# Which queue issues the loads: weights, sample cache and mixing operands from ScalarE instead of SyncE

## The chip, the cores and the metric

The kernel runs on one core of one Trainium2 chip. The metric is the device time of one execution in microseconds; the kernel before took 1886.35 us (median of 3 runs: 1886.35, 1886.42 and 1881.0).

A core has TensorE (PE in the profile; PEld are its weight loads), VectorE (DVE), ScalarE (ACT), GpSimd (POOL) and SyncE (SP). Each engine works off its own instructions in the order in which they stand in its program, and an instruction that waits holds back all that stand behind it on its engine. A transfer is also such an instruction: it is issued by an engine, in its place in that engine's program, and then runs on the 16 DMA engines. The profile writes SPq for transfers issued by SyncE.

## The reference, cut to what matters

One step of a hybrid decoder layer on 1024 prompt positions and 8 x 4 = 32 sample positions (T = 1056 columns in all), model width 2048. One input projection yields q, k, v, an attention gate, and u, vc and a gate for a chunked gMLP. Sixteen heads of 64 attend with three dilated causal windows, merged by their denominators; the sample rows also see a cache of 2048 past keys and values. The gated outputs go through an output projection, a residual and an RMSNorm.

```python
z = _rms_norm(x, norm_g) @ w_in
q, k, v, ga, u, vc, gb = jnp.split(z, SPLITS, axis=-1)
...
for window, d in DILATIONS:                     # (128, 1), (512, 4), (2048, 16)
    s = jnp.einsum('brnqhk,brnshk->brnhqs', qb, kcat) * scale
    p, lse = _softmax_lse(s, mask)
    o = jnp.einsum('brnhqs,brnshk->brnqhk', p, vcat)
return _combine(outs, lses)
...
mixed = jnp.einsum('gts,bcsgk->bctgk', _masked_spatial(w_s), vr) + jnp.transpose(b_s)[:, :, None]
return u * mixed.reshape(B, S, D_CHUNK)
...
a = o_attn.reshape(B, T, D_ATTN).astype(x.dtype) * jax.nn.silu(ga)
c = o_chunk * jax.nn.silu(gb)
return x + jnp.concatenate([a, c], axis=-1) @ w_out
```

## The kernel before, in words

**Projections.** Every product is made of fp16 parts: a float32 operand is split into a high part (ScalarE) and a low part (VectorE), and three matmuls replace one. The input projection has 56 tiles of 128 output columns, the output projection 16. A tile is three chunks of 352 positions (`proj_chunk`, L181), each of 48 matmuls: 144 a tile. Its weights come as two raw halves of 512 KB (`w_load`, tile `wraw`, three buffers, L120) and are split in four parts (`w_split`: `wh` on ScalarE L138, `wl` on VectorE L139). `run_m` loads the first half for the tile after next at a tile's start; the second half of tile m + 1 is loaded inside `w_split` of tile m, after its part 1.

**Steps between the matmuls.** All other work is cut into steps with a cost each (`set_steps`); after every 6 projection matmuls `fill` runs as many steps as their costs allow. This gives the program's order. The framework's scheduler then orders each engine's instructions by that priority and by when it believes their operands ready, and it puts an instruction with low priority ahead where an engine would else be idle.

**Periods.** Tiles of the input projection are grouped by head pair. From the first pair's end on, a period (six tiles at first, five in two of the last) projects gates, u and v of one pair (`run_m`), then the q/k halves of a pair, tiles x and y, side by side (`run_ab`, with the rotation `rope`, L470 to L477, after every chunk). Beside these matmuls run:
- the prompt's attention of the pair before, 16 items (8 query tiles x 2 heads), one a slot: `fa` makes scores (L611, L612, tile `s`), the row minimum (L620) and the exponential (ACT L632); `fb` normalizes, splits (`pn`, L146 and L147) and transposes the probabilities by DMA (`pt`, L648, four buffers); `fc` multiplies them with the values into the one PSUM bank `o` (L659, L666) and evacuates it (ACT `ot` L670, DVE `onat` L671). `fc` runs three slots after `fa`; `gate` (L677) follows when both heads are there.
- the sample's attention in x and y (`sample_steps`): `load` brings 8 key and 8 value blocks of 448 KB (`kvr`, two buffers, L712); `prep` splits one (keys `kvh` on ScalarE L720, values on GpSimd L722, then `kvl` on VectorE L723; three buffers each) and at its end loads the block after next; `s_mm` makes the scores (L751, L752), `soft1` and `soft2` the softmax (L774 to L799, ending in the DMA transposes `pst`), `pv_new` (L808) and `pv_mm` (L819, L820) the value products, `fin` the result.
- the mixing of the gMLP: `mix_load` brings eight pieces `vr` (L858) and three small operands (L867 to L869).
- at the end of `run_ab`, `stack_load` (L500 to L504) reads back the rotated q and k of the pair from DRAM into `qst`, `khd` and `klo`, with which the next prompt attention begins.

**Queues.** All transfers are issued by SyncE, in one order: loads, stores and DMA transposes.

Of the kernel before, what the change touches and what calls it, by code (L numbers as in the profile page):

```python
# [54 lines left out]
def hybrid_step_kernel(  # L55
# [25 lines left out]
    nc = tc.nc  # L81
    PE, ACT, DVE, POOL, SP = nc.tensor, nc.scalar, nc.vector, nc.gpsimd, nc.sync

    def pool(name, stack=ctx, bufs=1, **kw):
# [27 lines left out]
    def w_load(m, half=0, parts=1):  # L112
# [5 lines left out]
        for i in range(parts):  # L118
            c = slice(i * n, (i + 1) * n)
            SP.dma_start(  # L120
                out=t.rearrange("p a b -> p (a b)")[:, c], in_=src[:, half * KT * 64 + i * n:half * KT * 64 + (i + 1) * n]
            )
        w_raw[m, half] = t

    def w_split(m, part):
# [15 lines left out]
        )  # L141
        if part == 1:
            w_load(m + 1, 1)
# [442 lines left out]
    ap_ = pool("ap", right, side="right")  # L586
    msk = ap_.tile([64, NKEY + NS], F32, name="msk")
    trl = ap_.tile([128, 160], F32, name="trl")
    SP.dma_start(out=msk, in_=mask_s)
    SP.dma_start(out=trl, in_=tril)  # L590
# [4 lines left out]
    def prompt_steps(p):  # L595
# [90 lines left out]
        n = len(items)  # L686
        for s in range(n + 4):
            fs = []
            cost = 1.2 if s > 4 else 2.0
            if s - 4 >= 0 and (s - 4) % 2 == 1:  # L690
                fs.append(lambda t=(s - 4) // 2: gate(t))
            if 0 <= s - 3 < n:
                fs.append(lambda i=s - 3: fc(i))
                cost += 0.04 * (items[s - 3][0] + 1)
            if 0 <= s - 1 < n:
                fs.append(lambda i=s - 1: fb(i))
            if s < n:
                fs.append(lambda i=s: fa(i))
                cost += 0.04 * (items[s][0] + 1)
            slots.append((cost, lambda fs=fs: [f() for f in fs]))  # L700
        return slots, ahl

    def sample_steps(p, ahl):
        raws = {}
        sts = {}

        def load(j):
            if j >= 2 * DB:
                return
            t = ap_.tile([128, NKEY], F32, tag="kvr", name="kvr", bufs=2)  # L710
            src = kc if j < DB else vc
            SP.dma_start(out=t, in_=src[p, :, j % DB])  # L712
            raws[j] = t

        def prep(j):
# [10 lines left out]
            sts[j] = (hi, lo)  # L726
            load(j + 2)

        cur = {}

# [30 lines left out]
        def soft1():  # L761
            stsb = cur["st"]
            ss = ap_.tile([128, S], F32, tag="sp", name="ss", bufs=2)[0:64, 0:NKEY + NS]
            prev = 3e38
            for g in range(2):
# [17 lines left out]
                )  # L783
                prev = mn[0:64]
            den = ap_.tile([128, 1], F32, tag="den", name="den", bufs=6)
            ACT.activation(out=ss, in_=ss, func=AF.Exp, scale=-1.0, bias=prev, accum_out=den[0:64])
# [35 lines left out]
        def fin():  # L822
            o = cur["o"]
            a = ap_.tile([128, 64], F32, tag="oa", name="oa", bufs=1)
            b = ap_.tile([128, 64], F32, tag="ob", name="ob", bufs=1)
            ACT.activation(out=a, in_=o[:, 64:128], func=AF.Copy)
# [15 lines left out]

        pre = [(0.05, lambda: load(0)), (0.05, lambda: load(1))]
        s1 = [(0.1, lambda: prep(0)), (0.1, lambda: prep(1)), (0.2, s_new), wait(0.8)]
# [10 lines left out]
    def vr_load(g, half):  # L855
        vr = ap_.tile([128, 4, 2, 128], F16, tag="vr", name="vr", bufs=2)
        for i in range(4):
            SP.dma_start(out=vr[:, i], in_=vr_d[half * 4 + i, :, :, g * 128:(g + 1) * 128])  # L858
        return vr

    def mix_load(g):
# [4 lines left out]
        gs = slice(g * 128, (g + 1) * 128)  # L866
        SP.dma_start(out=vrs, in_=vr_d[NQ, 0:NS, :, gs])  # L867
        SP.dma_start(out=wr, in_=wst[g])
        SP.dma_start(out=bb, in_=bst[g].partition_broadcast(128))  # L869
        mixs[g] = (vr, vrs, wr, bb)  # L870
# [428 lines left out]
```

## Time and profile before

| | |
|---|---|
| median of 3 runs | 1886.35 us (1881.0 to 1886.42) |
| the profiled execution's own time | 1881.56 us |
| its span, first to last instruction | 1879.8 us |
| mean granted TensorE clock | 0.995 |
| TensorE busy | 1790.0 us (95%) |
| VectorE busy | 1085.5 us (58%) |
| ScalarE busy | 724.5 us (39%) |
| GpSimd busy | 125.2 us (7%) |
| transfers | 276.13 MB, 56.3% of 16 DMA engines' span on SyncE's queue |

Busy times don't count the issuing of transfers. Times within the execution are given in us from the span's start. In the view of waits a row names the engine and line that waited, what ended the wait, and the total in us, the number of times and the longest one. In the timeline a row has its start, its duration, engine, line, operation, output and inputs, a count, and in brackets the idle time of the engine before it and what ended it. A wait for several things is put down to the one that came last.

### The profile page before, as it was taken

To read this page: it belongs to the slowest core of one execution; us is meant where nothing else is said; L and a number is where in the kernel's file an instruction comes from. 1 tells how busy PE (TensorE), PEld (TensorE's weight loads), DVE (VectorE), ACT (ScalarE), POOL (GpSimd) and SP (SyncE) were. 2 spreads that over 40 slices of the span, in tenths; PEclk is the share of its full clock that TensorE was granted. 3 is DMA by queue.
4 is the path that set the end of the run, shared out by engine and by line. 5 is a ranking of instruction groups with operands and counts; after the bars stand their busy time and mean duration, and the time that the engine had idled before them with its cause. 6 is when DMAs were issued, how large, how long until landed. Compare 5 with 4: busy or idle time off the path is not lost. (4 is left out here: it accounts for less than half of the span.)

```text
span 1879.8 us, 37188 instructions
## 1 busy us (share of the span) xinstructions
PE 1790.0 (95%) x15040; PEld 1220.3 (65%) x15040; DVE 1085.5 (58%) x2392; ACT 724.5 (39%) x1605; POOL 125.2 (7%) x139
## 2 busy tenths in 40 slices
PE   8999998999999999999999999999989999999997
PEld 7866665666666666666666656666656666666667
DVE  7733696746665665665755566566566533324344
ACT  7522323632542453354244245245245311212134
POOL 0000010001001000100100100100100110000001
PEclk9999999999999999999999999999999999999999
DMA  7433346666656655656665666576675697222324
GB/s 260 118 81 68 81 135 184 122 166 172 147 117 180 180 120 162 191 115 154 172 157 125 160 202 116 149 210 130 165 197 110 178 336 190 68 68 68 77 59 185
DMA packets 340414, 276.13 MB, mean 147 GB/s; under 512 B 255889, under 2 KB 291729, under 8 KB 338129
## 3 DMA queue, kind: packets, MB, share of 16 engines
q1 hardware_dynamic: 340242, 273.76, 56.3%
q8 instruction: 117, 1.92, 0.4%
q14 instruction: 55, 0.45, 0.1%
HBM read 179.85 MB, written 38.26 MB: 116 GB/s over the span
## 5 line engine op out<-in xcount | busy, mean ns | idle before, releaser
L181 PE MATMUL proj<-xh,wh 128*128 128x352 f16 (+3 forms) x3712 | 1107.7, 303 | 6.2 <-DVE ta L475 2.9
L181 PE MATMUL proj<-xl,wh 128*128 128x352 f16 (+3 forms) x3712 | 1107.3, 303 | 1.5 <-DVE xl L147 1.5
L181 PE MATMUL proj<-xh,wl 128*128 128x352 f16 (+3 forms) x3712 | 1107.1, 303 | 0.4 <-DVE wl L139 0.4
L181 PEld LDWEIGHTS <-wh 128*128 128x128 f16 x7424 | 696.9, 98 | 325.4 <-issue 6.0
L181 PEld LDWEIGHTS <-wl 128*128 128x128 f16 x3712 | 362.6, 98 | 169.7 <-issue 1.9
L139 DVE SCALAR_TENSOR_TENSOR wl<-wraw,wh 128x512 f16<-128x512 f32 x288 | 202.3, 730 | 124.8 <-ACT wh L138 123.9
L138 ACT ACTIVATE wh<-wraw 128x512 f16<-128x512 f32 x288 | 165.8, 620 | 205.7 <-PE proj L181 198.7
L723 DVE SCALAR_TENSOR_TENSOR kvl<-kvr,kvh 128x896 f16<-128x896 f32 x128 | 143.0, 1117 | 95.3 <-ACT kvh L720 53.0
L632 ACT ACTIVATE sp<-sp,mn 128x256 f32<-128x256 f32 (+7 forms) x128 | 99.0, 773 | 150.6 <-DVE mn L620 150.6
L147 DVE SCALAR_TENSOR_TENSOR pn<-sp,pn 128x512 f16<-128x512 f32 (+2 forms) x192 | 106.4, 565 | 33.5 <-ACT pn L146 32.7
L722 POOL TENSOR_SCALAR kvh<-kvr 128x896 f16<-128x896 f32 x64 | 70.2, 1098 | 439.6 <-DMA kvr<-in_vc 272.2
L146 ACT ACTIVATE pn<-sp 128x512 f16<-128x512 f32 (+2 forms) x192 | 94.8, 516 | 11.4 <-DMA pt<-pn 8.4
L720 ACT ACTIVATE kvh<-kvr 128x896 f16<-128x896 f32 x64 | 60.7, 948 | 80.7 <-DMA kvr<-in_kc 46.4
L620 DVE CUSTOM_DVE_ANT_0 sp<-s,mp 128x512 f32<-128x512 f32 (+3 forms) x128 | 74.3, 584 | 21.6 <-PE s L612 20.1
L659 PE MATMUL o<-vst,pt 128*128 128x128 f16 x576 | 66.5, 220 | 21.0 <-DMA pt<-pn 17.4
L147 DVE SCALAR_TENSOR_TENSOR yhl<-proj,yhl 128x352 f16<-128x352 f32 (+1 forms) x42 | 21.4, 510 | 92.3 <-ACT yhl L146 92.3
L146 ACT ACTIVATE yhl<-proj 128x352 f16<-128x352 f32 (+1 forms) x42 | 18.8, 448 | 135.9 <-PE proj L181 116.5
L659 PEld LDWEIGHTS <-pt 128*128 128x128 f16 x576 | 52.1, 98 | 28.5 <-DMA pt<-pn 18.5
L639 DVE RECIPROCAL r<-den 128x1 f32<-128x1 f32 x128 | 20.8, 162 | 81.1 <-ACT sp L632 80.9
L666 PE MATMUL o<-vst,pt 128*128 128x64 f16 x576 | 63.0, 193 | 0.0
L923 POOL TENSOR_TENSOR gb<-gb,tb 128x352 f32<-128x352 f32 x24 | 28.8, 1201 | 511.4 <-DVE tb L203 511.4
L611 PE MATMUL s<-khd,qst 128*128 128x512 f16 (+2 forms) x192 | 61.7, 327 | 0.9 <-DVE mn L620 0.9
(165 smaller groups left out, 1562.6 us busy)
## 6 DMA issues: line engine op xcount, KB each, us to landing
wraw<-in_w_in SPq DMA_DIRECT2D x110, 512.0 KB, 4.5
kvr<-in_kc SPq DMA_DIRECT2D x64, 448.0 KB, 4.3
kvr<-in_vc SPq DMA_DIRECT2D x64, 448.0 KB, 4.0
wraw<-in_w_out SPq DMA_DIRECT2D x32, 512.0 KB, 5.1
yn<-in_x SPq DMA_DIRECT2D x8, 1024.0 KB, 9.2
out_y_p<-yn SPq DMA_DIRECT2D x16, 512.0 KB, 3.5
xn<-in_x SPq DMA_DIRECT2D x7, 1024.0 KB, 6.4
out_v_o<-tb SPq DMA_DIRECT2D x24, 176.0 KB, 2.5
```

What stands on the lines that cost most here:

```text
L138: ACT.activation(out=hi[:, sl, :], in_=r[:, rs, :], func=AF.Copy, scale=WS)
L139: DVE.scalar_tensor_tensor(out=lo[:, sl, :], in0=r[:, rs, :], scalar=WS, in1=hi[:, sl, :], op0=ALU.mult, op1=ALU.subtract)
L146: ACT.activation(out=hi, in_=src, func=AF.Copy, scale=scale)
L147: DVE.scalar_tensor_tensor(out=lo, in0=src, scalar=scale, in1=hi, op0=ALU.mult, op1=ALU.subtract)
L181: PE.matmul(out=ps[:, 0:n], lhsT=a[:, k, :], rhs=b[:, k, c0:c0 + n], start=(i == 0), stop=(i == 3 * KT - 1))
L611: PE.matmul(out=ps[:, 0:n], lhsT=qst[h][:, tq], rhs=khd[h][:, j0:j0 + n], start=True, stop=False)
L620: DVE.tensor_tensor_reduce(sp[:, j0:j0 + n], ps[:, 0:n], mp[:, S - nk + j0:S - nk + j0 + n], 1.0 / (QS * KS), prev, ALU.add, ALU.min, mn,)
L632: ACT.activation(out=sp[:, 0:nk], in_=sp[:, 0:nk], func=AF.Exp, scale=-1.0, bias=prev, accum_out=den)
L659: PE.matmul(out=o[:, 0:128].rearrange("p (l c) -> p l c", l=2), lhsT=pt[:, j], rhs=vst[:, :, kb, h * HD:(h + 1) * HD], start=(kb == 0), st ...
L666: PE.matmul(out=o[:, 0:64], lhsT=pt[:, w + j], rhs=vst[:, 0, kb, h * HD:(h + 1) * HD], start=False, stop=(kb == nb - 1))
L722: POOL.tensor_scalar(hi, r, VS, 1.0, ALU.mult, ALU.mult)
L723: DVE.scalar_tensor_tensor(out=lo, in0=r, scalar=KS if j < DB else VS, in1=hi, op0=ALU.mult, op1=ALU.subtract)
```

## The change

- The weight loads from the fifth tile on, the sample's key and value loads and the mixing loads are issued by ScalarE (`LQ`), at the places in its program where the scheduler puts them. Stores, DMA transposes and the loads of `stack_load` stay on SyncE.
- The second raw half of the weights is loaded after part 3 of the split instead of part 1.
- `kvr` gets a third buffer, so three key blocks are loaded ahead, and a `prep` of a key block loads the third block after it. The mask of the sample's softmax has no buffer of its own any more: it is loaded every period as the ninth block, into a `kvr` buffer. Three value blocks (the third to the fifth) are loaded by `soft1`, between its minima and its exponential, the last three by the preps of the third to the fifth.
- In the prompt attention, `fc` of the items 0 to 7 comes one slot later (four after `fa`), those of the items 8 to 15 stay at three, so that slot 11 has two (items 7 and 8). `gate` comes one slot later everywhere.
- In `fin` two small tiles share buffers with `ot` (left out below).

```diff
--- before.py
+++ after.py
@@ -80,6 +80,7 @@
 ):
     nc = tc.nc
     PE, ACT, DVE, POOL, SP = nc.tensor, nc.scalar, nc.vector, nc.gpsimd, nc.sync
+    LQ = ACT
 
     def pool(name, stack=ctx, bufs=1, **kw):
         return stack.enter_context(tc.tile_pool(name=name, bufs=bufs, **kw))
@@ -117,7 +118,7 @@
         n = KT * 64 // parts
         for i in range(parts):
             c = slice(i * n, (i + 1) * n)
-            SP.dma_start(
+            (SP if m < 4 else LQ).dma_start(
                 out=t.rearrange("p a b -> p (a b)")[:, c], in_=src[:, half * KT * 64 + i * n:half * KT * 64 + (i + 1) * n]
             )
         w_raw[m, half] = t
@@ -139,7 +140,7 @@
         DVE.scalar_tensor_tensor(
             out=lo[:, sl, :], in0=r[:, rs, :], scalar=WS, in1=hi[:, sl, :], op0=ALU.mult, op1=ALU.subtract
         )
-        if part == 1:
+        if part == 3:
             w_load(m + 1, 1)
 
     def hilo(src, hi, lo, scale):
@@ -584,9 +585,7 @@
 
     right = ExitStack()
     ap_ = pool("ap", right, side="right")
-    msk = ap_.tile([64, NKEY + NS], F32, name="msk")
     trl = ap_.tile([128, 160], F32, name="trl")
-    SP.dma_start(out=msk, in_=mask_s)
     SP.dma_start(out=trl, in_=tril)
 
     def wait(c):
@@ -684,14 +683,15 @@
 
         slots = []
         n = len(items)
-        for s in range(n + 4):
+        for s in range(n + 5):
             fs = []
             cost = 1.2 if s > 4 else 2.0
-            if s - 4 >= 0 and (s - 4) % 2 == 1:
-                fs.append(lambda t=(s - 4) // 2: gate(t))
-            if 0 <= s - 3 < n:
-                fs.append(lambda i=s - 3: fc(i))
-                cost += 0.04 * (items[s - 3][0] + 1)
+            if s - 5 >= 0 and (s - 5) % 2 == 1:
+                fs.append(lambda t=(s - 5) // 2: gate(t))
+            for i in range(n):
+                if s == i + (4 if i < 8 else 3):
+                    fs.append(lambda i=i: fc(i))
+                    cost += 0.04 * (items[i][0] + 1)
             if 0 <= s - 1 < n:
                 fs.append(lambda i=s - 1: fb(i))
             if s < n:
@@ -703,14 +703,19 @@
     def sample_steps(p, ahl):
         raws = {}
         sts = {}
+        cur = {}
 
         def load(j):
-            if j >= 2 * DB:
+            if j > 2 * DB:
                 return
-            t = ap_.tile([128, NKEY], F32, tag="kvr", name="kvr", bufs=2)
+            t = ap_.tile([128, NKEY + NS], F32, tag="kvr", name="kvr", bufs=3)
+            if j == DB:
+                LQ.dma_start(out=t[0:64], in_=mask_s)
+                cur["msk"] = t
+                return
             src = kc if j < DB else vc
-            SP.dma_start(out=t, in_=src[p, :, j % DB])
-            raws[j] = t
+            LQ.dma_start(out=t[:, 0:NKEY], in_=src[p, :, j if j < DB else j - DB - 1])
+            raws[j if j < DB else j - 1] = t[:, 0:NKEY]
 
         def prep(j):
             hi = ap_.tile([128, NKEY], F16, tag="kvh", name="kvh", bufs=3)
@@ -724,9 +729,10 @@
                 out=lo, in0=r, scalar=KS if j < DB else VS, in1=hi, op0=ALU.mult, op1=ALU.subtract
             )
             sts[j] = (hi, lo)
-            load(j + 2)
-
-        cur = {}
+            if j < DB:
+                load(j + 3)
+            elif j >= DB + 2:
+                load(j + 4)
 
         def s_new():
             stsb = cur["st"] = ap_.tile([128, NKT + 1, 64], F32, tag="stp", name="stsb", bufs=1)
@@ -760,6 +766,7 @@
 
         def soft1():
             stsb = cur["st"]
+            msk = cur["msk"][0:64]
             ss = ap_.tile([128, S], F32, tag="sp", name="ss", bufs=2)[0:64, 0:NKEY + NS]
             prev = 3e38
             for g in range(2):
@@ -782,6 +789,8 @@
                     mn[0:64],
                 )
                 prev = mn[0:64]
+            for i in (3, 4, 5):
+                load(DB + i)
             den = ap_.tile([128, 1], F32, tag="den", name="den", bufs=6)
             ACT.activation(out=ss, in_=ss, func=AF.Exp, scale=-1.0, bias=prev, accum_out=den[0:64])
             r = ap_.tile([128, 1], F32, tag="r", name="r", bufs=6)
...
@@ -840,7 +849,7 @@
             hilo(f[:, 0:NS], ahl[:, 0, S:T], ahl[:, 1, S:T], AS)
             SP.dma_start(out=act_d[p], in_=ahl)
 
-        pre = [(0.05, lambda: load(0)), (0.05, lambda: load(1))]
+        pre = [(0.05, lambda: load(0)), (0.05, lambda: load(1)), (0.05, lambda: load(2))]
         s1 = [(0.1, lambda: prep(0)), (0.1, lambda: prep(1)), (0.2, s_new), wait(0.8)]
         for b in range(DB):
             s1.append((0.4, lambda b=b: (s_mm(b), prep(b + 2))))
@@ -855,7 +864,7 @@
     def vr_load(g, half):
         vr = ap_.tile([128, 4, 2, 128], F16, tag="vr", name="vr", bufs=2)
         for i in range(4):
-            SP.dma_start(out=vr[:, i], in_=vr_d[half * 4 + i, :, :, g * 128:(g + 1) * 128])
+            LQ.dma_start(out=vr[:, i], in_=vr_d[half * 4 + i, :, :, g * 128:(g + 1) * 128])
         return vr
 
     def mix_load(g):
@@ -864,9 +873,9 @@
         wr = ap_.tile([128, 160], F32, tag="wr", name="wr", bufs=1)
         bb = ap_.tile([128, 160], F32, tag="bb", name="bb", bufs=1)
         gs = slice(g * 128, (g + 1) * 128)
-        SP.dma_start(out=vrs, in_=vr_d[NQ, 0:NS, :, gs])
-        SP.dma_start(out=wr, in_=wst[g])
-        SP.dma_start(out=bb, in_=bst[g].partition_broadcast(128))
+        LQ.dma_start(out=vrs, in_=vr_d[NQ, 0:NS, :, gs])
+        LQ.dma_start(out=wr, in_=wst[g])
+        LQ.dma_start(out=bb, in_=bst[g].partition_broadcast(128))
         mixs[g] = (vr, vrs, wr, bb)
 
     def mix_prep(g):
```

**ScalarE, the sample's softmax** (period of the fourth pair's x and y; `sa` are the two halves of the scores' sums, `ss` the exponential, `pn` its high part, `qkhl` the rotation's high part of a chunk). Before:

```order
L756 ACTIVATE sa<-s 128x224
L720 ACTIVATE kvh<-kvr 128x896 x3
L756 ACTIVATE sa<-s 128x224
L146 ACTIVATE qkhl<-o_9428 128x704
L786 ACTIVATE ss,den<-ss,mn 64x928
L146 ACTIVATE pn<-ss 64x928
L146 ACTIVATE qkhl<-o_9578 128x704
L138 ACTIVATE wh<-wraw 128x512 x4
```

Now:

```order
L762 ACTIVATE sa<-s 128x224
L147 ACTIVATE qkhl<-o_9428 128x704
L717 DMA kvr<-in_vc 128x896 x3
L795 ACTIVATE ss,den<-ss,mn 64x928
L717 DMA kvr<-in_vc 128x896
L147 ACTIVATE pn<-ss 64x928
L147 ACTIVATE qkhl<-o_9584 128x704
L717 DMA kvr<-in_vc 128x896 x2
L139 ACTIVATE wh<-wraw 128x512 x4
L121 DMA wraw<-in_w_in 128x1024 x2
```

Three value loads now stand ahead of the exponential and one between it and the high part of the probabilities. That one takes the buffer of the third value block, and waits for its `kvl`.

**VectorE, the same place.** Before:

```order
L774 ISA ss,mn<-t,msk,mn 64x416
L774 ISA mn 64x1
L788 RECIPROCAL r<-den 64x1
L789 TENSOR_SCALAR ss<-ss,r 64x928
L147 SCALAR_TENSOR_TENSOR pn<-ss,pn 64x928
```

Now:

```order
L781 ISA ss,mn<-t,kvr,mn 64x416
L781 ISA mn 64x1
L728 SCALAR_TENSOR_TENSOR kvl<-kvr,kvh 128x896
L471 TENSOR_TENSOR ta<-proj,cos_t 128x352
L797 RECIPROCAL r<-den 64x1
L798 TENSOR_SCALAR ss<-ss,r 64x928
L148 SCALAR_TENSOR_TENSOR pn<-ss,pn 64x928
```

The `kvl` of the third value block and one operation of the rotation have come between the minimum and the reciprocal.

**SyncE, the first prompt attention** (`pt` are the transposes of the probabilities). Before:

```order
L590 DMA trl<-in_tril 128x160
L858 DMA vr<-vr_d 128x2x128 x8
L867 DMA vrs<-vr_d 32x2x128
L868 DMA wr<-in_wst 128x160
L869 DMA bb<-in_bst 128x160
L648 DMA_TRANSPOSE pt<-pn 128x2x128 x2
L120 DMA wraw<-in_w_in 128x1024 x2
L648 DMA_TRANSPOSE pt<-pn 128x4x128
L712 DMA kvr<-in_kc 128x896 x2
```

Now:

```order
L437 DMA vr_d<-gnat 256x1x1024 x2
L589 DMA trl<-in_tril 128x160
L647 DMA_TRANSPOSE pt<-pn 128x2x128 x2
L647 DMA_TRANSPOSE pt<-pn 128x4x128 x2
L647 DMA_TRANSPOSE pt<-pn 128x6x128 x2
```

The transposes follow one another; the eleven mixing loads now stand on ScalarE, ahead of the first two exponentials of the prompt attention (L631), and nothing but transposes is left between those of `pt`.

**TensorE.** Three places differ, counted in projection matmuls. The last `pv_mm` of a period stood 20 matmuls after the end of tile y and now stands 9 before it. The first score of the next prompt attention (`khd`) stood 107 matmuls after the end of tile y, now 86. The value products of items 7 and 8 stood 24 matmuls apart (period of the third pair's attention), now 10. The places of `s_mm`, of `soft1`'s transposes and of `pv_new` are the same but for the last `s_mm`, which stands 3 to 11 matmuls earlier; from the transposes to `pv_new` it is 72 matmuls in both.

More of the change, by code (lines that the diff above doesn't have):

```diff
@@ L823, in fin @@
             o = cur["o"]
-            a = ap_.tile([128, 64], F32, tag="oa", name="oa", bufs=1)
-            b = ap_.tile([128, 64], F32, tag="ob", name="ob", bufs=1)
+            a = ap_.tile([128, 64], F32, tag="ot", name="oa", bufs=2)
+            b = ap_.tile([128, 64], F32, tag="ot", name="ob", bufs=2)
             ACT.activation(out=a, in_=o[:, 64:128], func=AF.Copy)
```

## The prediction

> **What bounds the kernel now.** I read the page first, then the waits of TensorE, then the timeline around each kind of wait.
>
> ```profile
> span 1879.8 us, 37188 instructions
> PE 1790.0 (95%) x15040; PEld 1220.3 (65%) x15040; DVE 1085.5 (58%) x2392; ACT 724.5 (39%) x1605; POOL 125.2 (7%) x139
> ```
>
> TensorE sets the time: it is busy for 1790.0 of 1879.8 us, so at most 89.8 us can be had by better order. The change alters no matmul. What it can win or lose are TensorE's waits.
>
> ```profile
> PE o L659 <- DMA pt<-pn: 17.4, 12, 4.9
> PE o L819 <- POOL kvh L722: 9.4, 7, 2.4
> PE o L808 <- DMA pst<-pn: 9.4, 8, 2.1
> PE s L751 <- ACT kvh L720: 7.9, 10, 1.8
> PE o L820 <- DVE kvl L723: 7.0, 10, 1.6
> PE s L752 <- DVE kvl L723: 6.0, 7, 0.9
> PE t L677 <- DVE onat L671: 4.7, 3, 1.7
> PE o L659 <- DVE onat L671: 1.7, 1, 1.7
> ```
>
> These eight rows hold 63.5 us, and all of them lie in the attention stages that the change touches. The rest is the start, the end and single waits, which it leaves alone. One period looks like this (TensorE's timeline, rows with an idle time; s is the sample's scores, o its value products or the prompt's):
>
> ```profile
> 732.33 0.18 PE L752 MATMUL s<-qbd,kvl 128*128 128x8 f16 x1 [0.94 <-DVE kvl L723]
> 736.85 0.18 PE L751 MATMUL s<-qbd,kvh 128*128 128x16 f16 x1 [0.54 <-ACT kvh L720]
> 754.79 0.22 PE L808 MATMUL o<-pst,vsn 32*128 32x128 f16 x1 [0.74 <-DMA pst<-pn]
> 767.15 0.18 PE L820 MATMUL o<-pst,kvl 128*128 128x8 f16 x1 [0.71 <-DVE kvl L723]
> 772.62 0.18 PE L819 MATMUL o<-pst,kvh 128*128 128x16 f16 x1 [0.45 <-POOL kvh L722]
> ```
>
> Each is under 1 us: every chain is late by a little. So a small shift of a chain removes its wait, or makes one.
>
> **What the loads cost where they are issued.** The view by tile gives the issues (minimum, median and maximum in ns), and at its end the time to landing, here for `kvr`:
>
> ```profile
> L712 SPq DMA_DIRECT2D kvr<-in_vc x64: 327/345/543, 412.3 to 1514.9; - x64
> DMA to landing us min/median/max: 3.3/4.0/6.8
> ...
> L120 SPq DMA_DIRECT2D wraw<-in_w_in x114: 327/398/1515, 2.5 to 1433.9; - x114
> ...
> L858 SPq DMA_DIRECT2D vr<-vr_d x64: 541/606/1337, 305.7 to 1466.7; - x64
> ...
> L648 SPq DMA_TRANSPOSE pt<-pn x192: 1167/1232/2567, 313.3 to 1455.4; - x192
> ```
>
> ScalarE takes over 136 weight issues (of 146, those of the first tiles stay), 136 of `kvr` with the mask, and 88 for the mixing: 136 x 0.40 + 136 x 0.345 + 88 x 0.61 = about 155 us. With its 724.5 us busy that is 47% of the span, so ScalarE has room on the whole. What counts is where an issue holds the work behind it.
>
> **Term 1, the sample's preparations.** Today's loads wait on SyncE until a buffer is free, and behind each other. In the same period:
>
> ```profile
> 732.30 0.33 SPq L712 DMA_DIRECT2D kvr<-in_kc  x1
> 735.85 0.95 ACT L720 ACTIVATE kvh<-kvr 128x896 f16<-128x896 f32 x1 [3.52 <-DMA kvr<-in_kc]
> ...
> 767.12 0.33 SPq L712 DMA_DIRECT2D kvr<-in_vc  x1
> 771.63 0.94 POOL L722 TENSOR_SCALAR kvh<-kvr 128x896 f16<-128x896 f32 x1 [5.48 <-DMA kvr<-in_vc]
> ```
>
> The last key block is issued at 732.30 and split 3.55 us later; the last value block at 767.12, 4.5 us before its split, and TensorE pays 0.54 and 0.45 us for them. With three buffers, six key blocks are loaded before `s_mm` begins and the seventh is issued when the fourth is split, so the split follows `s_mm`'s release of `kvh` instead of the load. The eighth value block is issued after `kvl` of the fifth, about 10 us earlier than now. The 0.71 us of `kvl` come from four splits of weights that stand ahead of it on VectorE; in the new order the sixth value block is already ahead of them. Of 7.9 + 6.0 us I leave 2, of 9.4 + 7.0 us I leave 3: a gain of 25 us (ends: 12, if VectorE's order keeps half, and 30).
>
> **Term 2, the prompt's transposes.** At the first prompt attention (SyncE's timeline, then TensorE's):
>
> ```profile
> 305.66 5.80 SPq L858 DMA_DIRECT2D vr<-vr_d  x8
> 313.33 2.51 SPq L648 DMA_TRANSPOSE pt<-pn  x2
> ...
> 316.56 0.27 PE L659 MATMUL o<-vst,pt 128*128 128x128 f16 x1 [4.89 <-DMA pt<-pn]
> ```
>
> The mixing loads hold the first two transposes until 313.33. Now they hold ScalarE for the same time, 8 x 0.61 + 3 x 0.6 = 6.7 us, ahead of the first two exponentials, so the transposes start no earlier; but the product comes one slot later, and no load stands between the later transposes. I halve this place's waits (4.9 + 2.1 + 1.3 us): a gain of 4. The other 9 us of the first row are the first products of the later periods, under 3 us each, and a slot of over 4 us covers them: a gain of 9, 13 in all (ends 5 and 17). `gate` one slot later covers the 4.7 us of `onat`: a gain of 4 (ends 2 and 4.7).
>
> **Term 3, new waits.** Four are to be weighed.
>
> First, the sample's softmax. ScalarE and VectorE today (timeline):
>
> ```profile
> 742.87 0.79 ACT L146 ACTIVATE qkhl<-o 128x704 f16<-128x704 f32 x1 [3.91 <-DVE o L477]
> ...
> 748.78 0.15 DVE L788 RECIPROCAL r<-den 64x1 f32<-64x1 f32 x1 [1.23 <-ACT ss L786]
> 749.70 0.98 ACT L146 ACTIVATE pn<-ss 64x928 f16<-64x928 f32 x1 [0.95 <-DVE ss L789]
> ```
>
> In the new order the reciprocal stands behind `kvl` of the third value block, whose load is issued only after `qkhl`, and `pn` behind a load that waits for the same `kvl`. From the end of `qkhl`, 743.7: landing 4.0, GpSimd 0.95, `kvl` 1.09, a rotation step 0.5: 750.2 instead of 748.8, so 1.5 us later. Against this, `s_mm` loses 1.5 us of waits before it, and `kvl` of the second block no longer stands between the two minima (1.1 us). I take `pst`'s 9.4 us as unchanged: 0 (ends: 9 us won; 8 periods x 1.5 = 12 lost).
>
> Second, the first scores of a prompt attention (TensorE, then SyncE):
>
> ```profile
> 787.91 0.22 PE L611 MATMUL s<-khd,qst 128*128 128x128 f16 x1
> ...
> 778.81 0.36 SPq L120 DMA_DIRECT2D wraw<-in_w_in  x1
> 779.27 0.37 SPq L486 DMA_DIRECT2D q_d<-qkhl  x1
> ...
> 784.68 0.59 SPq L504 DMA_DIRECT2D klo<-k_d  x1
> ```
>
> The transfer `klo` takes 3.4 us, so it lands at 788.1, and TensorE uses it at 788.56: no wait, and no slack. Now the scores stand 21 matmuls earlier. Matmuls of 352 columns start every 0.15 us:
>
> ```profile
> 959.69 0.31 PE L181 MATMUL proj<-xh,wh 128*128 128x352 f16 x1
> 959.84 0.31 PE L181 MATMUL proj<-xl,wh 128*128 128x352 f16 x1
> ```
>
> That is 3.1 us earlier, and 0.7 more since the waits after tile y are gone. SyncE gains the weight load that blocked `q_d` (0.8), and VectorE reaches the low part some 1.4 us sooner: 2.2 us. The difference, 1.6 us, seven times, is a loss of 11 (ends 0 and 7 x 3.8 = 27).
>
> Third, the products of items 7 and 8. Bank `o` is single, and the one case of two products close together cost 1.7 us (the last row of the waits). Ten matmuls, 1.5 us, lie between, against `ot` (0.32) and `onat` (0.28) and what stands ahead of `ot` on ScalarE, two weight issues among it: a loss of 1 us, eight times, 8 (ends 0 and 14).
>
> Fourth, ScalarE's issues beside its other work. The weight issues wait for `wl`, four splits of 0.69 us; behind them stand `ot`, exponentials and evacuations. Evacuations have cover: three banks, a chunk of 48 x 0.15 = 7.2 us each. The eight `vr` pieces delay one `ot` a period by 2.4 us, of which the slot takes 2. I take 5 lost (ends 0 and 20).
>
> Nothing else is on the path: transfers are 56% of the DMA engines' time and no byte is added but 7 masks of 232 KB.
>
> **Sum.** 25 + 13 + 4 gained, 0 + 11 + 8 + 5 lost: 18 us net. The profiled execution took 1881.56 us (span 1879.8): 1863.5. Its time is 4.8 us below the median of the runs shown, 1886.35, whose values lie at 1881 and 1886; I start from their middle, 1883, and forecast 1865 for the changed kernel, 1.1% below 1886.35.
>
> **Rivals.**
> - *The new waits don't come* (terms 1 and 2 as summed, none of term 3): 42 gained, 1841. For it: waits of today are under 1 us, so the order fits the chip well. Against it: `klo` has no slack.
> - *The waits only move.* `kvl`, VectorE's order and the new waits take back what the loads release: terms 1 to 2 at their low ends, 12 + 5 + 2 = 19 against the 24 lost in the sum, or fewer: 1883 to 1888, no change.
> - *ScalarE is held in the softmax*, the slower side. Place: the load between exponential and `pn`. If the third value block lands in 6.8 us (the row's maximum) instead of 4.0, the chain to `pst` is 1.5 + 2.8 = 4.3 us longer, and eight periods cost 34 us: 34 - 18 = 16 us slower than before, 1899. It decides from 2.3 us a period on (18 / 8).
> - *Two queues delay each other's issues.* The trace shows one issuing queue only. Transposes of 1.23 us, 192 of them between 313 and 1455 us, fill 21% of that time. If an issue on ScalarE has to wait for one under way, 21% of 360 issues wait 0.6 us: 45 us of ScalarE's time, a seventh of it at places that TensorE waits for, 6 us: 1871.
>
> The page "Perfetto Trace Analysis" of the Trainium skill, section "DMA Instruction — HWDGE (DVE, Sync)", states such a rule: the descriptor generator is shared by the two sequencers and locked for one at a time, and the wait for the lock is part of the issue's profiled time. No run here shows it yet. By that rule the fourth rival's time holds; without it, the sum's.
>
> **How the numbers follow.** Forecast 0.42, no new waits 0.18, waits only move 0.17, held in the softmax 0.15, delayed issues 0.08. From no change, a measurement of this kernel can tell about 0.3%, 5.7 us: 1880.7 to 1892. Faster: 0.42 + 0.18 + 0.07 + 0.02 = 0.69 less 0.01 for the forecast's upper tail, 0.68; same 0.14; slower 0.18. The forecast's own range is 1850 to 1879. With the first rival below and half of the slower one above, I give 1838 to 1892.
>
> **What would show it.** Right: the rows of L751, L752, L819 and L820 in TensorE's waits fall from 30.3 to about 5 us, that of `pt` to about 4; new rows at L611 or L612 for `khd` or `klo` (about 11 us) and at L659 for `onat` (about 8); `pst` near 9. Issues on ScalarE keep medians near 0.35, 0.40 and 0.61 us; the fourth rival would lift them. The third would lift `pst` above 25 us. The forecast is wrong if a wait stands at L181 for an evacuation or a split, which would mean that ScalarE's holds reach the projections.

## The result, and the profile after

The change makes the kernel slower: 1950.87 us (median of 4 runs, 1943.84 to 1960.55) against 1884.59 us for the kernel before beside it, a ratio of 1.0358 (95% interval 1.0304 to 1.0412). I had forecast 1865. The profiled execution took 1960.55 us, the longest of the four, and that of the kernel before 1881.56, close to the shortest of its runs (1881.0); so the two profiles lie 79 us apart where the medians lie 66 us apart.

First the page of the changed kernel, then TensorE's waits (us in total, times, longest us):

```profile
span 1958.1 us, 37184 instructions
PE 1822.5 (93%) x15040; PEld 1236.9 (63%) x15040; DVE 1091.1 (56%) x2392; ACT 720.9 (37%) x1605; POOL 120.7 (6%) x139
```

```profile
PE s L610 <- DMA khd<-k_d: 41.6, 7, 6.3
PE o L658 <- DVE onat L670: 23.3, 16, 3.5
PE o L829 <- DVE kvl L728: 11.1, 7, 1.8
PE o L817 <- DMA pst<-pn: 7.9, 2, 7.5
PE o L658 <- DMA pt<-pn: 5.8, 4, 3.1
PE o L658 <- ACT ta L196: 5.6, 1, 5.6
PE s L758 <- DVE kvl L728: 5.5, 7, 0.9
PE s L757 <- ACT kvh L725: 5.4, 4, 2.2
...
PE proj L182 <- DVE wl L140: 3.1, 2, 2.7
...
PE o L828 <- POOL kvh L727: 1.6, 1, 1.6
```

The span is 78.3 us longer, and the two parts can be read off. TensorE idles 135.6 us instead of 89.8: 45.8 more. And it is busy 1822.5 us instead of 1790.0, with the same 15040 matmuls: 32.5 more. The busy part is the clock, the speed that TensorE is granted. In these traces it is either full (1.00) or half (0.50), and the view of cores gives a mean of 0.970 against 0.995 before. One place shows how it is lost (TensorE's row, then the view by windows: us, PE busy with its instructions, granted clock, DMA share, GB/s):

```profile
820.93 0.26 PE L610 MATMUL s<-khd,qst 128*128 128x128 f16 x1 [5.92 <-DMA khd<-k_d]
```

```profile
821.00:826.00 5.00, 5.00 (x19) 0.50 0.57 152
826.00:836.00 10.00, 10.00 (x72) 1.00 0.25 51
```

TensorE waits 5.92 us for the first scores' `khd`. In the 5 us behind the wait the clock is half: 19 instructions recorded, where the window behind it runs 72 in 10 us. So this place costs about 6 us of waiting and some 2.5 us of slow work. There are seven like it, one at each prompt attention but the first; they are the first row of the waits, and that row was not there before.

Why is `khd` late? SyncE's timeline around the same place, with the DMA view of 806 to 821 us (the queues with packets, MB and share of 16 engines, SyncE's q1 and ScalarE's q10; issues with the KB of each and the median us to landing):

```profile
807.30 1.76 SPq L487 DMA_DIRECT2D q_d<-qkhl  x3
...
810.47 0.45 SPq L488 DMA_DIRECT2D k_d<-qkhl  x1
814.01 0.34 SPq L501 DMA_DIRECT2D qst<-q_d  x1
...
814.99 0.59 SPq L504 DMA_DIRECT2D khd<-k_d  x1
```

```profile
q10 hardware_dynamic: 678, 2.31, 50.1%
q1 hardware_dynamic: 1212, 1.34, 32.8%
...
kvr<-in_kc ACTq DMA_DIRECT2D x3, 448.0 KB, 5.4
wraw<-in_w_in ACTq DMA_DIRECT2D x2, 512.0 KB, 5.7
...
khd<-k_d SPq DMA_DIRECT2D x4, 128.0 KB, 6.4
...
q_d<-qkhl SPq DMA_DIRECT2D x4, 40.0 KB, 4.9
```

q and k go out to DRAM (`q_d`, `k_d`) and come back (`qst`, `khd`). SyncE has issued its last write at 810.47 and stands until 814.01, since `q_d` has not landed; the `khd` issued at 814.99 is used at 820.93. In those 15 us ScalarE's queue moves 2.31 MB beside SyncE's 1.34. The rest of this document tests whether that is the cause.

### The profile page after: what moved, and what is told of

It reads as the page before. It is cut to its first block, busy times and chain, and to the rows that moved or that the text cites. A ratio compares the mean times of both kernels' runs of the same rounds, so it can differ in the third digit from the quotient of the medians.

```text
span 1958.1 us, 37184 instructions
## 1 busy us (share of the span) xinstructions
PE 1822.5 (93%) x15040; PEld 1236.9 (63%) x15040; DVE 1091.1 (56%) x2392; ACT 720.9 (37%) x1605; POOL 120.7 (6%) x139
## 5 line engine op out<-in xcount | busy, mean ns | idle before, releaser
L182 PE MATMUL proj<-xh,wh 128*128 128x352 f16 (+3 forms) x3712 | 1121.7, 307 | 6.2 <-DVE ta L476 3.6
L182 PE MATMUL proj<-xh,wl 128*128 128x352 f16 (+3 forms) x3712 | 1121.3, 307 | 3.1 <-DVE wl L140 3.1
L182 PE MATMUL proj<-xl,wh 128*128 128x352 f16 (+3 forms) x3712 | 1120.4, 306 | 1.4 <-DVE xl L148 1.4
L182 PEld LDWEIGHTS <-wh 128*128 128x128 f16 x7424 | 703.6, 99 | 340.1 <-issue 7.8
L182 PEld LDWEIGHTS <-wl 128*128 128x128 f16 x3712 | 366.3, 99 | 181.2 <-DVE wl L140 4.0
L631 ACT ACTIVATE sp<-sp,mn 128x256 f32<-128x256 f32 (+7 forms) x128 | 99.1, 774 | 212.8 <-DVE mn L619 199.4
L638 DVE RECIPROCAL r<-den 128x1 f32<-128x1 f32 x128 | 20.9, 163 | 90.0 <-ACT sp L631 89.8
L665 PEld LDWEIGHTS <-pt 128*128 128x128 f16 x576 | 50.9, 98 | 30.5 <-issue 27.0
L658 PEld LDWEIGHTS <-pt 128*128 128x128 f16 x576 | 52.5, 99 | 17.0 <-DMA pt<-pn 6.9
```

The source lines that it names most:

```text
L182: PE.matmul(out=ps[:, 0:n], lhsT=a[:, k, :], rhs=b[:, k, c0:c0 + n], start=(i == 0), stop=(i == 3 * KT - 1))
L631: ACT.activation(out=sp[:, 0:nk], in_=sp[:, 0:nk], func=AF.Exp, scale=-1.0, bias=prev, accum_out=den)
L658: PE.matmul(out=o[:, 0:128].rearrange("p (l c) -> p l c", l=2), lhsT=pt[:, j], rhs=vst[:, :, kb, h * HD:(h + 1) * HD], start=(kb == 0), st ...
L665: PE.matmul(out=o[:, 0:64], lhsT=pt[:, w + j], rhs=vst[:, 0, kb, h * HD:(h + 1) * HD], start=False, stop=(kb == nb - 1))
```

## The experiments

Two theories at the start. **A**: loads on a second queue run beside the round trip of q and k and lengthen it; one queue in order had kept them apart. **B**: the scheduler put the first scores 21 projection matmuls earlier (83 behind the end of tile y instead of 104; the description of the change counts 86 and 107, the same distance), and that alone makes the wait.

### The loads back on SyncE, all or in part

```diff
-    LQ = ACT
+    LQ = SP
```

> All loads of the change back on SyncE's queue; the third cache buffer, the mask in it, the later weight load and the later slots stay. The first scores of a prompt attention stand 85 projection matmuls behind the end of tile y, against 83 in the change and 104 in the kernel before. Two theories of the 6 us that TensorE waits for khd, seven times, in the change. Theory A (shared DMA engines): the round trip of q and k through DRAM takes longer because loads of a second queue run beside it (khd landing 6.4 us in the change, 3.6 before); with one queue the landing goes back to about 3.6, the wait to at most 19 x 0.15 = 2.9 us a time (under 20 us in sum against 41.6), so short that no half clock follows, TensorE busy about 1790: 1870 to 1890 us. Theory B (early scores alone): the scores stand too early whatever the queue; landing is not the cause, the wait stays at 5 to 6 us a time, about 40 in sum, with the half clock behind it: 1935 to 1950 us.

Measured: 1887.07 us, ratio 1.0019 (1.0005 to 1.0032). So moving the loads to ScalarE carries some 64 of the 66 us (1950.87 - 1887.07); buffer, mask and slots together cost 3. (The queue alone, on the kernel before, was not run.) Its page, TensorE's waits, and the DMA view of 769.5 to 784.5 us, which ends 1.2 us ahead of the first score at 785.65:

```profile
PE 1794.1 (95%) x15040; PEld 1226.0 (65%) x15040; DVE 1085.2 (58%) x2392; ACT 723.2 (38%) x1605; POOL 123.9 (7%) x139
```

```profile
PE s L610 <- DMA khd<-k_d: 16.4, 9, 3.7
PE o L658 <- DVE onat L670: 15.8, 12, 2.3
...
PE o L829 <- DVE kvl L728: 7.4, 7, 1.4
...
PE s L758 <- DVE kvl L728: 1.9, 3, 0.9
```

```profile
q1 hardware_dynamic: 1789, 3.43, 73.7%
...
khd<-k_d SPq DMA_DIRECT2D x3, 128.0 KB, 3.4
...
q_d<-qkhl SPq DMA_DIRECT2D x4, 40.0 KB, 2.0
```

The DMA engines move somewhat less in such a stage: 3.31 MB in the 15 us up to the first score, and 2.90 MB if the 15 us are laid at the last write of `k_d` as in the change's window, against 2.31 + 1.34 there. With one queue the cache loads and the write of the attention's result stand ahead of the round trip, and `q_d` lands in 2.0 us instead of 4.9, `khd` in 3.4 instead of 6.4. Theory A's numbers came; B's 40 us of waiting did not. What is left, 16.4 us, is the share of the earlier scores (buffer_scores_100 below, with one queue and the scores put back, has 1.3).

The other two put one kind of load back:

```diff
-            (SP if m < 4 else LQ).dma_start(      # weights_on_sync
+            SP.dma_start(
...
-            LQ.dma_start(out=t[:, 0:NKEY], in_=src[...])   # cache_on_sync, and the mask
+            SP.dma_start(out=t[:, 0:NKEY], in_=src[...])
```

> Weight loads back on SyncE, cache and mixing loads stay on ScalarE. The scheduler then puts the first scores 98 matmuls behind tile y, 6 (0.9 us) earlier than before. Theory A: the cache loads of ScalarE still run beside the round trip, khd landing about 5 us, waits of 1.5 to 3 us a time, 10 to 20 in sum, little half clock: 1885 to 1910 us. Theory B: 0.9 us early gives under 1 us a time, under 7 in sum, landing no matter: 1865 to 1885 us.

> Cache loads and mask back on SyncE, weights and mixing loads stay on ScalarE. First scores 100 matmuls behind tile y, 4 (0.6 us) earlier than before. Theory A: two or three weight loads of 512 KB beside the round trip, khd landing about 5 us, waits of 1 to 3 us a time, 7 to 20 in sum: 1880 to 1905 us. Theory B: under 0.6 us a time, 4 in sum: 1865 to 1885 us. The sample's value splits then wait for their loads again as before (7 to 9 us each row).

Measured: 1905.21 us (1.0112, 1.0082 to 1.0143) with cache and mixing on ScalarE, and 1945.87 us (1.0324, 1.0296 to 1.0351) with weights and mixing on ScalarE. The `khd` rows are 29.4 and 39.1 us in seven places. Here the scheduler put the scores at 98 and 100 matmuls, nearly where they stood before, and the waits are still 3 to 7 us each: B alone is out. My forecast under A fell short, too: I had expected 7 to 20 us of waits. From the timelines I took the steps of the chain, medians of the seven places, from ScalarE's high split of the last chunk to the first score:

| kernel | split to last `k_d` issue | to `qst` issue | to second `khd` issue | to first score | sum | TensorE waits |
|---|---|---|---|---|---|---|
| before | 3.67 | 2.56 | 0.97 | 4.30 | 11.8 | none |
| change | 3.42 | 3.53 | 1.01 | 6.48 | 14.6 | 5.5 to 6.3 |
| one_queue | 3.25 | 0.54 | 1.00 | 3.31 | 8.4 | 0.9 to 3.7 |
| weights_on_sync | 4.26 | 4.35 | 0.97 | 3.25 | 13.3 | 3.2 to 5.7 |
| cache_on_sync | 6.19 | 1.85 | 0.92 | 3.60 | 12.7 | 4.6 to 7.2 |

Each mixture lengthens another step: with cache loads on ScalarE the writes land late (4.35), with weights there SyncE issues the writes late (6.19): a cache load stands among them, and the writes of `k_d` wait for earlier writes to land (1.7 us in the stage of 804 to 815 us). The median landing of `khd` over the whole run is 3.3 and 3.5 us in these two, no longer than before (3.6): a median over one transfer hides where the chain is late.

### The slots alone

```diff
-            if 0 <= s - 3 < n:
-                fs.append(lambda i=s - 3: fc(i))
+            for i in range(n):
+                if s == i + (4 if i < 8 else 3):
+                    fs.append(lambda i=i: fc(i))
```

(on the kernel before, with `gate` one slot later as in the change)

> The kernel before with only the later slots (value products of items 0 to 7 one slot later, gate one slot later); all loads as before. First scores at 104 matmuls as before, so no wait for khd by either theory. My prediction's terms: pt 17.4 to about 4, gate's onat 4.7 to 0, against 8 new for onat at items 7 and 8: 9 us faster, about 1875. The change's own trace says otherwise: onat 23.3 us, 3.5 us at each first double product, pt 5.8: net 5 us slower, about 1890, and more if half clock follows the 3.5 us gaps.

Measured: 1903.93 us, 1.0111 (1.0082 to 1.0141). The slots lose 20 us where I had them gain 9. The profile is of the quickest of the four executions, 1895.57 us, and shows some 14 of the 20. The waits (us in total, times, longest), and the two places of one period:

```profile
PE o L659 <- DVE onat L671: 22.9, 15, 2.5
...
PE o L659 <- DMA pt<-pn: 8.9, 9, 2.5
```

```profile
832.39 0.22 PE L659 MATMUL o<-vst,pt 128*128 128x128 f16 x1 [1.58 <-DVE onat L671]
869.80 0.22 PE L659 MATMUL o<-vst,pt 128*128 128x128 f16 x1 [2.27 <-DVE onat L671]
```

`pt` falls from 17.4 to 8.9 and `onat` rises from 1.7 to 22.9. The wait at 832.39 is the one of items 7 and 8 in the single bank `o`, as foreseen. The one at 869.80 was not: there, a product of the last tile waits for `ot` and `onat` of the product before it, which stand behind the mixing's `chl` split on ScalarE and VectorE.

### The buffer alone, and loads added to the kernel before

one_queue with the slots of the kernel before:

```diff
-    LQ = ACT
+    LQ = SP
...
-                if s == i + (4 if i < 8 else 3):
+                if s == i + 3:
```

> Of the change only the third cache buffer with the mask in it, the later weight load and the shared small buffer; all loads on SyncE, slots as before. If the parts add up (one_queue 1887, the later slots alone 20 us slower than before), this is 1867 us, with 16 us of khd waits left (first scores at 85 matmuls) and 'onat' back to about 2 us at the value products. If the slots cost what they do only with the old buffers, it stays at 1885 or above.

Measured: 1879.98 us, 0.9977 (0.9957 to 0.9996): 0.2% faster, with an interval that ends just below 1. The parts do not add up; the slots cost 7 us here and 20 on the kernel before. The sample's waits do what I had said of them:

```profile
PE s L610 <- DMA khd<-k_d: 14.9, 7, 3.3
...
PE o L829 <- DVE kvl L728: 9.5, 9, 1.5
...
PE s L757 <- ACT kvh L725: 0.8, 1, 0.8
```

With a row of 0.5 us for L758 and none for L828 the four rows of the sample's preparations hold 10.8 us, against 30.3 before: the third buffer wins 19.5 us. Most of that goes again: 14.9 to the first scores, which the scheduler has moved from 104 to 85 matmuls, and smaller pieces to `klo` (2.9), `gate` (8.5 instead of 4.7) and one first product (4.1).

Next, A's cause by itself, on the kernel before and with TensorE's order unchanged. The added transfers are copies of cache blocks from DRAM to an unused place in DRAM, so they read and write there, where the change's loads only read:

```diff
         hilo(o12, hl[:, 0], hl[:, 1], QS)
+        if c0 + n > S and 0 < p < 6:
+            for jj in range(4):
+                tc.keep_in_program_order(ACT.dma_start(out=junk[jj], in_=kc[p - 1, :, jj]))
```

> The kernel before, TensorE's order untouched (scores at 104 matmuls), with four copies of 448 KB of cache rows into an unused scratch in DRAM, issued on ScalarE just behind the high split of the last chunk of q and k, in periods 1 to 5 only; periods 6 and 7 have none. Theory A (loads beside the round trip lengthen it): from the high split to the first score 11.8 us becomes 14 to 16, khd waits of 2 to 4 us at five places and none at the last two: 10 to 20 us, 1895 to 1910 us in all. Rival (it is ScalarE being held, or the scheduler's order): four issues hold ScalarE for 4 x 0.35 us, and no wait for khd comes: 1880 to 1890 us.

Measured: 1908.82 us, 1.0132 (1.0101 to 1.0163). TensorE's rows with a wait for `khd` of more than 1 us, the first and the last of five:

```profile
471.81 0.27 PE L615 MATMUL s<-khd,qst 128*128 128x128 f16 x1 [3.51 <-DMA khd<-k_d]
...
1127.13 0.27 PE L615 MATMUL s<-khd,qst 128*128 128x128 f16 x1 [3.96 <-DMA khd<-k_d]
```

Five waits, at the five places with added loads, and none at the two without: the chain from split to score grew from 11.8 to 15.5 us there (15.2 to 15.9). So transfers beside the round trip are enough by themselves. Two rows on the third place, from the DMA view of 783 to 799 us and from the view by tile of the added loads:

```profile
q_d<-qkhl SPq DMA_DIRECT2D x4, 40.0 KB, 5.5
```

```profile
ACT ahl L147: 25.8, 5
```

`q_d` lands in 5.5 us there, against 3.1 in the same stage of the kernel before. The second row is something that I had not wanted: the added issues held ScalarE for 5 us at each place, and the small split `ahl` behind them came late. It is not the 4 x 0.35 us that I had expected. The chain of q and k has no work on ScalarE after its high split, but SyncE's write of `ahl` stands between the writes and the reads of q and k, so the hold could have reached the reads. It did not: at four of the five places that write was issued within 0.8 us of the last `k_d` (2.4 us at the first), and at all five the reads behind it were issued another 2.4 to 3.3 us later, when transfers had landed.

### Scores later, loads held back

```diff
-        return [wait(1.5)] + pr
+        return [wait(20.0)] + pr
...
-            run_m(MG[g], head_start(pr[:5]), ga_evac)
+            run_m(MG[g], head_start(pr[:4]), ga_evac)
```

(and the first score matmuls of items 0 and 1 pinned to the order of the program)

> The change with its loads on ScalarE, but the first scores of a prompt attention held back to 108 matmuls behind tile y instead of 83 (25 x 0.15 = 3.75 us later), four slots instead of five in the first tile. The khd wait should fall from 6 to about 2.2 us a time, 42 to 16 us in sum. If the gaps cost only themselves: 26 us less, 1925 us. If a gap of 6 us also takes half the clock from the next 7 us and one of 2 us does not: another 20 to 30 us less, TensorE busy about 1795 to 1800 instead of 1822: 1895 to 1905 us.

Measured: 1939.29 us, 1.0298 (1.0262 to 1.0335). The gap shrank as said, to 1.5 to 3.2 us at the first scores, 26.4 us in sum with the second ones. The clock did not come back: TensorE is busy 1818.8 us. TensorE's rows at one period, and the window that begins between them:

```profile
643.28 0.22 PE L610 MATMUL s<-khd,qst 128*128 128x128 f16 x1 [2.77 <-DMA khd<-k_d]
646.92 0.27 PE L610 MATMUL s<-khd,qst 128*128 128x128 f16 x1 [1.98 <-DMA khd<-k_d]
```

```profile
645.40:652.20 6.80, 5.28 (x20) 0.51 0.13 30
```

Two gaps of 2 to 3 us close together cost the clock as much as one of 6 us does. My expectation that short gaps are free of it fell.

The opposite way leaves the scores at 85 matmuls and takes the loads out of the round trip, still on ScalarE's queue:

```diff
-            LQ.dma_start(out=t[:, 0:NKEY], in_=src[...])
+            tc.keep_in_program_order(LQ.dma_start(out=t[:, 0:NKEY], in_=src[...]))
...
-        w_load(m + 2)
...
             evac(proj_chunk(m, c0, n), c0, n)
+            if ci == 1:
+                w_load(m + 2)
```

> The change with all its loads on ScalarE, but none in the round trip: weight and cache loads are pinned to the order of the program on ScalarE, and a tile's weight load is issued behind its second chunk instead of at its start. First scores at 85 matmuls. Theory A (what runs beside the round trip, not which queue issues it): the legs from k_d to qst and from khd to the score go back from 3.5 and 6.5 us to about 0.6 and 3.4, the khd wait from 42 to about 16 us as in one_queue; with the half clock of these gaps gone, 1890 to 1910 us. Rival (a second issuing queue slows SyncE's transfers or its issues whenever both are in use): legs and khd wait stay, about 1950 us.

Measured: 1940.71 us, 1.0302 (1.0264 to 1.034). Its waits, and the DMA view of 876 to 886 us, where a prompt attention ends:

```profile
PE o L661 <- DMA pt<-pn: 54.0, 21, 5.6
...
PE s L613 <- DMA khd<-k_d: 1.2, 2, 1.0
```

```profile
q1 hardware_dynamic: 2528, 0.97, 59.8%
q10 hardware_dynamic: 1303, 0.92, 30.0%
...
pt<-pn SPq DMA_TRANSPOSE x1, 7.3
```

The chain takes 8.3 us again, as with one queue, and the `khd` waits are gone with both queues in use: it is what runs beside it that counts, not which engine issues. But the time did not come back. The loads that left the round trip now run beside the prompt's transposes. `pt` lands in up to 12.5 us (6.7 before), and TensorE waits 54.0 us for it where it had waited 17.4.

The same with the slots of the kernel before:

```diff
-                if s == i + (4 if i < 8 else 3):
+                if s == i + 3:
```

> loads_held with the slots of the kernel before. If the slots cost 20 us here too, as between the kernel before and slot_alone: 1870 to 1890 us, with onat at the value products back under 3 us. If the slots' cost was hidden behind khd waits: no difference to loads_held.

Measured: 1936.97 us, 1.028 (1.025 to 1.031). `onat` leaves the list at the products, `pt` takes its place with 63.3 us. The two runs lie within 4 us of each other, so here the slots' cost is mostly hidden, behind the transposes.

### What is left of the change that helps

buffer_alone with the edit of scores_later; then with a smaller wait, and the first attention left alone; and buffer_alone with the mixing loads on ScalarE:

```diff
-        return [wait(1.5)] + pr                      # buffer_scores_later
+        return [wait(20.0)] + pr
...
-        return [wait(1.5)] + pr                      # buffer_scores_100
+        return [wait(16.0)] + pr
...
-                a2 = head_start(pr[:5]) + a2
+                a2 = [wait(1.5)] + pr[:4] + a2
...
-            (SP if m < 4 else LQ).dma_start(         # mixing_on_scalar, on the change
+            SP.dma_start(                            # (cache and mask likewise)
```

> buffer_alone with the first scores held back to 108 matmuls. The khd waits of 16 us vanish: about 1852 us, faster than both kernels, if the later slots keep their distances; if the denser slots behind bring new waits for pt or onat (10 to 15 us), 1862 to 1870 us.

Measured: 1883.04 us, 0.9999 (0.9983 to 1.0016). `khd` is down to 1.8 us, but the first attention, held back too, waits 7.0 us at once, and the slots behind are denser (`pt` 13.8).

> buffer_alone with the first scores of periods 1 to 7 at 102 matmuls instead of 85, the first attention left as in buffer_alone. khd and klo 18 us in buffer_alone to about 3; the 7 us gap at the first attention of buffer_scores_later gone: 1868 us if pt and onat stay at 20 us in sum, 1880 if they grow as in buffer_scores_later.

Measured: 1877.02 us, 0.9955 (0.9939 to 0.9972): faster than both kernels, by 0.45% against the one before, little, but with an interval that lies below 1. It has the third buffer, all loads on SyncE, the old slots, and `wait(16.0)` with four slots from period 1 on.

> buffer_alone with the mixing loads alone on ScalarE (88 issues). First scores at 85 matmuls. In the kernel before, the first attention's transposes wait behind eight mixing loads (8.4 us for its pt waits in sum); freed of them 3 to 5 us, and no load of 448 KB or more beside the round trip, so khd as in buffer_alone: 1873 to 1880 us. If any load on ScalarE lengthens the round trip, khd rises above 25 us: 1890 us or more.

Measured: 1886.65 us, 1.001 (0.9997 to 1.0023), 7 us over buffer_alone. `khd` stays at 14.1, the first attention still waits 5.2 us for `pt`: as the prediction said of this place, the loads then hold ScalarE's exponentials for as long.

## Why the prediction was wrong

Its sum, term by term, in the profiled executions:

| term | forecast | measured in the change | with one queue |
|---|---|---|---|
| 1, sample preparations | 25 won | 6.7 won | 20.7 won |
| 2, `pt` | 13 won | 11.6 won, 5.6 lost to `ta` in its place | 14.1 won, 3.4 lost to `sp` |
| 2, `gate` | 4 won | 4.7 won | 0.4 lost |
| 3, the softmax's `pst` | 0 | 1.5 won | 4.4 lost |
| 3, first scores | 11 lost | 42.5 lost | 17.4 lost |
| 3, items 7 and 8 (`onat`) | 8 lost | 21.6 lost | 14.1 lost |
| clock (TensorE busy) | not in the sum | 32.5 lost | 4.1 lost |

**The step that failed** is the second part of term 3. Its mechanism was there: no slack at `klo`, scores moved 21 matmuls forward. With one queue it costs 17.4 us, within its ends of 0 and 27. What the step had wrong is that it let the round trip get shorter (2.2 us, from SyncE's and VectorE's order), while term 3 ended with "Nothing else is on the path: transfers are 56% of the DMA engines' time". With one queue it does get shorter, 8.4 us instead of 11.8; in the change it gets longer, 14.6. The 5.0 us between 2.2 shorter and 2.8 longer, seven times, are 35 us; with the 11 forecast that is 46, and 42.5 were measured. An average share says nothing of the 15 us in which the chain needs the engines: there they are 83% busy in the change (50.1 + 32.8) and 71 to 74% with one queue, and the change put 2.31 MB of a second queue among the short transfers. one_queue, loads_beside_round_trip and loads_held show that from three sides. The Trainium skill, "DMA: Bandwidth & Descriptors", section "Issuing engines are not separate DMA queues", states that transfers of all issuing engines interleave on the same 16 DMA engines. The traces agree: in the change's 15 us the two queues take 50.1% and 32.8% of the same 16 engines, and `q_d` lands in 4.9 us instead of 2.0. It was the rule to weigh against this change; I weighed the one on the descriptor generator instead.

**The clock** was not a term at all, and is 32.5 us. Before the change the waits are so short that it rarely shows. In the change TensorE is busy for 85.5 us at half clock in all (10.8 before); half of the difference, 37 us, is about what its busy time grew by. In the stretches at the seven `khd` waits it is 28.7 us, so the clock took some 14 us there, 2 a place. The rest stands behind the other waits, for `onat`, `pt`, `pst` and the sample's preparations above all.

**Term 1** was right for the buffer and wrong for the queue. The preparations' waits fall to 9.6 us with one queue and only to 23.6 in the change, where the cache loads share with all others, and `kvl` of the values waits behind VectorE's weight splits all the same (11.1 us).

**Items 7 and 8** held in kind: 1.3 us a place in the change and 1.6 in slot_alone (medians), against 1 forecast. A second place at the attention's end, not foreseen, more than doubles it in the change. Since in slot_alone both together (21.2 us) outweigh `pt`'s gain (8.5), the slots are a loss on the kernel before.

**The rivals.** The slower one, ScalarE held in the softmax, did not come: `pst` is 7.9 us, not above 25, and 7.5 of it stand at one place in the last period. Its direction, slower, came by another mechanism. The fourth, queues that delay each other's issues, is not seen in the change either: the weights' issues on ScalarE (view by tile, ns: minimum, median, maximum) are no longer than SyncE's were (327/398/1515).

```profile
L121 ACTq DMA_DIRECT2D wraw<-in_w_in x104: 329/334/393, 83.1 to 1506.8; - x104
```

One of them, 0.34 us long, starts at 84.36, in the midst of a transpose's issue on SyncE (1.24 us from 83.97), and is not held up by it. By the rule of the Trainium skill that the prediction cites for this rival, a wait for the lock would be part of the issue's time; these issues show none.

The projections saw one new wait at L182 for a split, 2.7 us at 242.60: small, but of the kind that the prediction named as a sign of being wrong. It stands in cache_on_sync too and not in one_queue.

## What to carry to other kernels

Here one in-order queue was also an order of precedence on the shared DMA engines. Before bulk loads leave it for a second queue, list the short chains through memory that TensorE waits for (here q and k through DRAM, and the transposes), with their slack, and count the bytes that will run beside them in those microseconds, not the mean share of the span. And where waits grow past a microsecond or two, add to the price the half clock that can follow them.

## What the hardware showed that was not expected

A gap's length does not decide whether the half clock follows. In the change a single wait of 1.80 us at 627.86 brought it (TensorE's row, then the windows ahead of it and behind it):

```profile
627.86 0.18 PE L829 MATMUL o<-pst,kvl 128*128 128x8 f16 x1 [1.80 <-DVE kvl L728]
```

```profile
624.69:628.10 3.41, 1.61 (x32) 1.00 0.53 161
628.10:631.50 3.40, 3.40 (x22) 0.50 0.86 250
```

while a wait of 3.46 us in one_queue left the clock full:

```profile
1249.65 0.22 PE L610 MATMUL s<-khd,qst 128*128 128x128 f16 x1 [3.46 <-DMA khd<-k_d]
```

```profile
1244.55:1247.96 3.41, 1.64 (x11) 1.00 0.62 172
1247.96:1251.37 3.41, 1.72 (x13) 1.00 0.78 230
1251.37:1258.00 6.63, 5.98 (x43) 1.00 0.78 246
```

What decides is how much of a gap falls into one step of 3.41 us. In all fourteen traces the stretches at half clock begin on a fixed grid of that step and, but for those at the program's end, last whole steps. The wait of 3.46 us lies across two steps, with 1.77 and 1.69 us idle; that of 1.80 us lies in one. Over all steps at full clock (the first three of a trace left aside), one with 2.0 us or more without a matmul was followed by half clock in 123 of 123 cases, one with 1.5 to 2.0 us in 25 of 120, and one with less in 1 of some 7300. What separates the cases between 1.5 and 2.0 us is open. So a wait of 2 to 3.5 us can cost the clock in one place and not in the next. The Trainium skill, "TensorE: Matmul & The Clock Gate", section "Why this matters for your kernels", asks for no idle gap above about 3 us; by these rows a shorter gap can halve the clock and a longer one can leave it full.

Also unexpected: the round trip is shorter with the changed buffers on one queue (8.4 us) than in the kernel before (11.8), although part of the 11.8 is slack that TensorE does not wait for. With one queue the write of the attention's result and a weight load stand ahead of the last chunk's writes, where in the kernel before the load stands among them and the write between them and the reads. That fits, but no run isolates it. The scheduler's earlier scores are thus not wholly wrong; with one queue they ask for 0.9 to 3.7 us more than the chain gives.
